# A decoder block on one core: weight buffers shared by both halves of the program, x loaded behind w_out, three down products accumulated in another's PSUM banks, a shorter row-norm chain

## The chip, the cores and the metric

The kernel runs on one core of one Trainium2 chip. The metric is the device time of one execution in microseconds (us); the time before is the median of three runs. A profile is one more execution, recorded by the hardware profiler. Its times are counted from the start of its span.

## The reference

One layer of a hybrid decoder on 512 tokens of width 1024, all in float32:

```python
h = rmsnorm(x, norm_attn_g)
q, k, v, u_pool, u_gate = split(h @ w_in)
a = diff_attention(q, k, v)          # 8 heads, rope, two softmaxes, w = p0 - lam * p1, rmsnorm per head
p = multiscale_pool(u_pool)          # causal means over 2, 4, 8, 16 tokens, then w_pool per group
merged = sigmoid(g_A) * a + sigmoid(g_P) * p
x = x + merged @ w_out
h2 = rmsnorm(x, norm_mlp_g)
x = x + square(relu(h2 @ w_up)) @ w_down        # 1024 -> 4096 -> 1024
return rmsnorm(x, final_norm_g)
```

## The kernel before

Every large product is made of three fp32r matmuls: each float32 operand is split into a rounded part (hi) and a rest (lo), and hi x hi, hi x lo and lo x hi are summed in PSUM. The weights come in tiles of 128 x 1024 float32 (512 KB, raw, `wr`), one DMA each on SP's queue (`get_w`, `load_w`). ScalarE casts a raw tile to its hi part `wh` (L109), then VectorE or GpSimd subtracts to get the lo part `wl` (L110). In the program's names a number behind a tile's name tells which one it is: `o0_2` is the third tile of the first half of w_out, `up0_3` the fourth w_up tile of quarter 0.

The order in which each engine takes its instructions is fixed when the program is built. A scheduler (`schedule_with_timeline_sim=True`) picks it from the dependences; tile pools decide which tiles share memory, and a tile that reuses memory waits for the last reader of the one before. Each engine, and SP's queue of DMA issues, works strictly in its order.

The stages, in order:
- The v projection, then attention: eight heads (`attn`), whose softmax chain runs over ScalarE and VectorE, with the gate projections (`ga`, `gp`) and the pooling as filler for TensorE. After each group of two heads `merge` applies the gates; its last step writes the merged tile as hi and lo part into `vh` and `vl` (L456, L457), which hold what w_out multiplies. The last group (heads 6 and 7) needs the last gate tile `gp7`, head 7's output `o7`, its norm (`ss`, L396, L397) and the pooled product `pp` (L451 to L453), whose weights `wpr` are loaded and split late; L454 takes pp out of PSUM.
- w_out, in two halves of 512 columns (n = 0 and 1, `po0` and `po1`), each of 8 x 3 matmuls for each of four token tiles t. Four weight tiles kk = 0 to 3 make up a half; tile kk covers heads 2 kk and 2 kk + 1. `x1_add` adds the result to x (L532) and squares it with a row sum (L514). After the second half come the row norm of h2 (L519, `rsqrt` L186 to L192, L553) and its transposes (L558), one token tile at a time.
- The MLP in four quarters q. `up(q)` has 8 weight tiles, each 24 matmuls; `down(q)` has 7 products of 24 matmuls in the order m1, m7, m6, m5, m2, m3, m4 (a Winograd-like scheme, whose weight operands `t1` to `t4` are sums of the loaded tiles, L629, and whose sums of results are made on VectorE in `accu` and in `x1`: U, V7 and V5 hold m1 + m6, m7 and m5 over the quarters).
- The final row norm, `finish` (L706), row by row in the last quarter, with output tiles `yo` from a pool tag `hy` of two buffers that squares and h2 use too.

Buffers for weights come from two pools. During attention `wp` has 3 raw tiles and 4 of hi and lo. `ctx1.close()` (L493) gives this memory and that of the attention tiles back, and a new pool `bk` takes it over, with 6 raw tiles and 4 of hi and lo (L495); its tiles wait for the old tiles in their place. The loads of x for the residual (L536) stand ahead of those of w_out.

Of the kernel before, what the change touches and what calls it, by code (L numbers as in the profile page):

```python
# [52 lines left out]
def block_kernel(ctx, tc, xT, x_tok, gains, pos, consts, w_in, w_v, w_pool, w_out, w_up, w_dn, out):  # L53
# [42 lines left out]
    def load_w(src, name, nsplit=1, parts=None):  # L96
        raw = wp.tile([P, 1024], F32, tag="wr", name=f"wr_{name}", bufs=wbufs[0])
        if nsplit == 1:
            nc.sync.dma_start(out=raw, in_=src)
# [409 lines left out]
    def hy(name):  # L509
        return bk.tile([P, D], F32, tag="hy", name=name, bufs=2)  # L510

    def square(t, n):

        A.activation(out=hy(f"sqj{t}_{n}")[:, :512], in_=x1[:, t, n * 512 : n * 512 + 512], func=AF.Square,  # L514
                     accum_out=st[:, t, n : n + 1])

    def row_scale(t):

        V.tensor_tensor(out=st[:, t, 2:3], in0=st[:, t, 0:1], in1=st[:, t, 1:2], op=ALU.add)  # L519
        rsqrt(st[:, t, 3:4], st[:, t, 2:3], st[:, t, 4:5], D)  # L520
        return st[:, t, 3:4]
# [25 lines left out]
    for t in range(NT):
# [5 lines left out]
        V.scalar_tensor_tensor(out=h2, in0=x1[:, t, :], scalar=row_scale(t), in1=g2b, op0=ALU.mult, op1=ALU.mult)  # L553
        for b in range(2):
            pt = acc(f"h2T{t}_{b}")
            for j in range(4):
                k = 4 * b + j
                T.transpose(out=pt[:, j * P : j * P + P], in_=h2[:, k * P : k * P + P], identity=ident)  # L558
# [50 lines left out]
    def down(q):  # L609
        def raw(b, name):  # L610
            out_ = []
            for c in range(2):
# [18 lines left out]
        def product(form, w, name, inner=True):
            pa = [acc(f"{name}{q}_{a}") for a in range(2)]
            order = [(p, a) for p in range(4) for a in range(2)] if inner else [(p, a) for a in range(2) for p in range(4)]
            for p, a in order:
# [3 lines left out]
                T.matmul(pa[a], lhsT=zh, rhs=hi[:, sl], start=p == 0, stop=False)  # L638
                T.matmul(pa[a], lhsT=zh, rhs=lo[:, sl], start=False, stop=False)  # L639
                T.matmul(pa[a], lhsT=zl, rhs=hi[:, sl], start=False, stop=p == 3)  # L640
            return pa

        def to_x1(pa, r, n, op=ALU.add):
            for a in range(2):
# [1 line left out]
                V.tensor_tensor(out=xs, in0=xs, in1=pa[a], op=op)  # L646

        def to_acc(pa, dst):
            for a in range(2):
                if q == 0:  # L650
                    A.copy(out=dst[:, a], in_=pa[a])
                else:
                    V.tensor_tensor(out=dst[:, a], in0=pa[a], in1=dst[:, a], op=ALU.add)
# [12 lines left out]
        for a in range(2):
            V.tensor_tensor(out=U[:, a], in0=m6[a], in1=U[:, a], op=ALU.add)
        comb(b12, b11, ALU.subtract)
        if last:
            for a in range(2):  # L670
                V.tensor_tensor(out=V7[:, a], in0=V7[:, a], in1=U[:, a], op=ALU.add)
            to_x1([V7[:, 0], V7[:, 1]], 1, 0)
        to_acc(product(S1, parts(b12, "t1", V), "m5"), V5)
        if last:
            for a in range(2):
                V.tensor_tensor(out=U[:, a], in0=U[:, a], in1=V5[:, a], op=ALU.add)
            to_x1([U[:, 0], U[:, 1]], 0, 1)
            for a in range(2):
                V.tensor_tensor(out=V7[:, a], in0=V7[:, a], in1=V5[:, a], op=ALU.add)
            to_x1([V7[:, 0], V7[:, 1]], 1, 1)  # L680
# [88 lines left out]
```

## Time and profile before

| | |
|---|---|
| median of three runs | 724.18 us (723.78 to 724.74) |
| profiled execution | 725.91 us, its span 724.1 us |
| mean granted TensorE clock | 0.981 |
| TensorE busy | 686.7 us (95%) in 3146 matmuls |
| VectorE, ScalarE, GpSimd busy | 516.8, 401.4, 276.0 us |
| HBM read | 70.94 MB, 101 GB/s over the span |

How to read what follows. A window's row gives its bounds and length, then the busy time and number of instructions of TensorE, its weight loads, VectorE, ScalarE and GpSimd, then the granted clock (1.00 is full), the share of the DMA engines, and GB/s. A timeline row gives the start, the duration, the engine, the line, the operation, the tiles out<-in, and in brackets how long the engine had idled and what ended that. PE is TensorE, PEld its weight loads, DVE VectorE, ACT ScalarE, POOL GpSimd, SPq SyncE's DMA queue; a line of groups has busy time and the mean ns of one behind the bar. In the waits, the total, the number and the longest stand behind the colon. Lines are those of the kernel before. Stages by time: v projection to 53 us, attention to 316, w_out with the row norm to 387, the MLP to 674 and on to its last matmul at 711.8, the final norm to 724.1.

### The profile page before, as it was taken

How to read it: one execution, taken by the hardware profiler on the slowest of the kernel's cores; microseconds unless marked ns; L12 is line 12 of the kernel's file. 1: busy time of each engine (PE TensorE's matmuls, PEld its weight loads, DVE VectorE, ACT ScalarE, POOL GpSimd, SP SyncE). 2: the span in 40 equal slices, each digit the busy share in tenths (PEclk: the TensorE clock that was granted, in tenths of full speed). 3: DMA queues.
4: the chain of work that ended last, by engine and by line, in shares of the span. 5: the costliest groups of instructions: out<-in, count | busy, mean ns of one | idle time of the engine just before them, and what ended most of it. 6: DMA issues, size and time to landing. Idle time of an engine off the chain costs nothing.

```text
span 724.1 us, 8745 instructions
## 1 busy us (share of the span) xinstructions
PE 686.7 (95%) x3146; PEld 567.1 (78%) x3146; DVE 516.8 (71%) x826; ACT 401.4 (55%) x661; POOL 276.0 (38%) x158
## 2 busy tenths in 40 slices
PE   8999999999999999967999999999999999999983
PEld 7888887787787877755888888888888888888872
DVE  6854998889899987945265886259833777259896
ACT  7553467874875768553355565356434564355424
POOL 6102623355335444404104314850465224850450
PEclk9999999999999999977999999999999999999997
DMA  8421322112311220056304314520264214520203
GB/s 269 161 103 58 117 84 82 48 61 81 100 59 58 79 75 0 2 215 233 110 31 123 110 58 155 194 88 30 88 209 151 76 59 149 197 90 29 88 30 117
DMA packets 22652, 73.61 MB, mean 102 GB/s; under 512 B 2768, under 2 KB 3408, under 8 KB 22608
## 3 DMA queue, kind: packets, MB, share of 16 engines
q1 hardware_dynamic: 22608, 73.05, 30.4%
q8 instruction: 25, 0.41, 0.2%
q14 instruction: 19, 0.16, 0.1%
HBM read 70.94 MB, written 2.10 MB: 101 GB/s over the span
## 4 chain that ended last, share of the span: by engine, by line
PE 57%; DVE 25%; ACT 10%; issue 4%; DMA 2%; POOL 2%; SPq 0%; DVEq 0%; ACTq 0%; POOLq 0%
PE pu L122 8%; PE pu L123 8%; PE pu L126 8%; PE m L639 6%; PE m L638 6%; PE m L640 6%; ACT p L367 2%; DVE p L372 2%; PE v L212 2%; PE v L213 2%; PE v L214 2%; PE po L527 2%; PE po L528 2%; DVE p L363 2%; PE po L526 2%
## 5 line engine op out<-in xcount | busy, mean ns | idle before, releaser
L110 POOL TENSOR_TENSOR wl_up<-wr_up,wh_up 128x1024 fp32r<-128x1024 f32 x30 | 74.3, 2481 | 75.6 <-ACT wh_up L109 60.1
L122 PE MATMUL pu<-x1gh,wh_up 128*128 128x512 f32 (+1 forms) x272 | 101.0, 377 | 0.2 <-ACT x1gh L561 0.2
L123 PE MATMUL pu<-x1gl,wh_up 128*128 128x512 f32 (+1 forms) x272 | 101.2, 377 | 0.0
L110 POOL TENSOR_TENSOR wl_t<-wr_b,wh_t 128x1024 fp32r<-128x1024 f32 x16 | 43.5, 2723 | 114.4 <-DVE zr L590 69.5
L126 PE MATMUL pu<-x1gh,wl_up 128*128 128x512 f32 (+1 forms) x272 | 63.8, 377 | 0.0
L122 PEld LDWEIGHTS pu<-x1gh,wh_up 128*128 128x128 f32 x272 | 51.0, 188 | 9.8 <-ACT x1gh L561 0.5
L123 PEld LDWEIGHTS pu<-x1gl,wh_up 128*128 128x128 f32 x272 | 51.1, 188 | 9.6 <-DVE x1gl L562 0.2
L367 ACT ACTIVATE p<-p,st 128x128 f32<-128x128 f32 (+3 forms) x64 | 35.7, 558 | 38.5 <-DVE st L363 38.2
L126 PEld LDWEIGHTS pu<-x1gh,wl_up 128*128 128x128 f32 x272 | 49.2, 188 | 9.3
L592 ACT CAST zfh<-zr 128x512 fp32r<-128x512 f32 (+1 forms) x32 | 30.3, 946 | 45.2 <-DVE zr L590 24.8
L629 DVE TENSOR_TENSOR wr_b<-wr_b,wr_b 128x1024 f32<-128x1024 f32 x32 | 48.0, 1507 | 5.7 <-DMA wr_b<-w_dn 5.5
L593 DVE TENSOR_TENSOR zfl<-zr,zfh 128x512 fp32r<-128x512 f32 (+1 forms) x32 | 38.5, 1203 | 18.0 <-ACT zfh L592 18.0
L109 ACT CAST wh_t<-wr_b 128x1024 fp32r<-128x1024 f32 x32 | 33.7, 1054 | 31.6 <-PE m L640 30.0
L109 ACT CAST wh_up<-wr_up 128x1024 fp32r<-128x1024 f32 x32 | 33.6, 1049 | 31.0 <-PE m L640 15.0
L639 PE MATMUL m<-wl_t,zfh 128*128 128x512 f32 x128 | 49.8, 389 | 0.0
L640 PE MATMUL m<-wh_t,zfl 128*128 128x512 f32 x128 | 49.8, 389 | 0.0
L638 PE MATMUL m<-wh_t,zfh 128*128 128x512 f32 x128 | 48.8, 389 | 0.0
L646 DVE TENSOR_TENSOR x<-x,m 128x512 f32<-128x512 f32 x30 | 20.2, 684 | 31.3 <-PE m L640 31.3
L639 PE MATMUL m<-wl_b,zfh 128*128 128x512 f32 x96 | 37.5, 390 | 2.4 <-DVE wl_b L110 2.4
L640 PE MATMUL m<-wh_b,zfl 128*128 128x512 f32 x96 | 37.4, 389 | 0.0
L638 PE MATMUL m<-wh_b,zfh 128*128 128x512 f32 x96 | 37.2, 389 | 0.0
L584 DVE TENSOR_TENSOR zr<-zr 128x256 f32<-128x256 f32 x16 | 15.6, 974 | 26.3 <-ACT zr L583 26.3
(257 smaller groups left out, 1874.0 us busy)
## 6 DMA issues: line engine op xcount, KB each, us to landing
wr_up<-w_up SPq DMA_DIRECT2D x32, 512.0 KB, 3.4
wr_b<-w_dn SPq DMA_DIRECT2D x32, 512.0 KB, 3.3
wr_q<-w_in SPq DMA_DIRECT2D x8, 512.0 KB, 3.3
wr_k<-w_in SPq DMA_DIRECT2D x8, 512.0 KB, 3.3
wr_ga<-w_in SPq DMA_DIRECT2D x8, 512.0 KB, 3.3
wr_gp<-w_in SPq DMA_DIRECT2D x8, 512.0 KB, 3.4
wr_o<-w_out SPq DMA_DIRECT2D x8, 512.0 KB, 6.5
wr_b22b<-w_dn SPq DMA_DIRECT2D x8, 512.0 KB, 3.3
```

The lines of the kernel that those rows point to most:

```text
L109: ins = A.copy(out=hi[:, sl], in_=raw[:, sl])
L110: (eng or G).tensor_tensor(out=lo[:, sl], in0=raw[:, sl], in1=f(hi)[:, sl], op=ALU.subtract)
L122: T.matmul(acc, lhsT=hi[:, c], rhs=rh[:, k, :], start=k == 0, stop=False)
L123: T.matmul(acc, lhsT=hi[:, c], rhs=rl[:, k, :], start=False, stop=False)
L126: T.matmul(acc, lhsT=lo[:, c], rhs=rh[:, k, :], start=False, stop=k == NK - 1)
L367: A.activation(out=pr[:, c, :N], in_=pr[:, c, :N], func=AF.Exp, scale=-1.0, bias=st[:, c : c + 1], accum_out=st[:, 2 + c : 3 + c])
L592: A.copy(out=zfh[:, sl, p, :], in_=F[:, sl])
L593: V.tensor_tensor(out=zfl[:, sl, p, :], in0=F[:, sl], in1=f(zfh)[:, sl, p, :], op=ALU.subtract)
L629: V.tensor_tensor(out=r1[c], in0=r1[c], in1=r2[c], op=op)
L638: T.matmul(pa[a], lhsT=zh, rhs=hi[:, sl], start=p == 0, stop=False)
L639: T.matmul(pa[a], lhsT=zh, rhs=lo[:, sl], start=False, stop=False)
L640: T.matmul(pa[a], lhsT=zl, rhs=hi[:, sl], start=False, stop=p == 3)
```

## The change

- The pool `wp` now lives to the end and serves both halves of the program, with 3 raw tiles and 4 of hi and lo. The w_down tiles `b12` and `b22`, which are combined in place, have four raw buffers of their own (`wr2`) in `bk`.
- The loads of x stand behind those of w_out's first half in the code.
- Three down products go on in the PSUM banks of another: m6 in m1's, m3 in m5's, m4 in m7's. So V7 and V5 are not needed: m1, m7 and m5 are added to x directly, the sum goes on in PSUM, and m4's sign is turned in its weights (`flip`). In the last quarter the splits of `b21` and `t4` are on VectorE.
- The row norm: for one half of the row the sum of squares is known early, and `row_early` makes of it a bias (two 128x1 operations); `row_scale` lets the logarithm take it, and the add of L519 goes. The squares' unused output goes into tiles that are there already; `hy` and `yo` go, `finish` works in place in x1, and of rows 2 and 3 the second half is multiplied by the gain ahead of time (VectorE) and scaled on ScalarE.

TensorE's order, at the end of attention. Before: the end of o7 (head 7's output), the sums of squares ss7 of its norm, the pooled products pp6 and pp7, then w_out's first half (`po0_0` is token tile 0):

```order
L384 MATMUL o7_2729<-wt_532,vh_107 128x128
L396 MATMUL ss7_2750<-sqh7_2744,onesr_88 128x512 [waits PE_49,Activation_49]
L397 MATMUL ss7_2750<-sql7_2746,onesr_88 128x512 [waits DVE_49]
L451 MATMUL pp6_2944<-dh3_2805,wt_532 128x512 [waits Activation_49]
L452 MATMUL pp6_2944<-dl3_2806,wt_532 128x512
L451 MATMUL pp7_2954<-dh3_2805,wt_532 128x512
L452 MATMUL pp7_2954<-dl3_2806,wt_532 128x512
L453 MATMUL pp6_2944<-dh3_2805,wt_532 128x512 [waits DVE_49]
L453 MATMUL pp7_2954<-dh3_2805,wt_532 128x512
L526 MATMUL po0_0_2976<-wh_o0_0_2982,vh_107 128x512 [waits DVE_49,Activation_49]
```

No matmul of w_out stood ahead of pp. Now, the same place (the lines are those of the changed kernel: L531 to L533 make po, L395 and L396 ss, L450 to L452 pp):

```order
L531 MATMUL po0_3_2975<-wh_o0_2_3038,vh_107 128x512
L395 MATMUL ss7_2750<-sqh7_2744,onesr_88 128x512 [waits PE_49,Activation_49]
L532 MATMUL po0_3_2975<-wl_o0_2_3039,vh_107 128x512
L533 MATMUL po0_3_2975<-wh_o0_2_3038,vl_108 128x512
L396 MATMUL ss7_2750<-sql7_2746,onesr_88 128x512 [waits DVE_49]
L450 MATMUL pp6_2944<-dh3_2805,wt_532 128x512 [waits Activation_49]
L451 MATMUL pp6_2944<-dl3_2806,wt_532 128x512
L450 MATMUL pp7_2954<-dh3_2805,wt_532 128x512
L451 MATMUL pp7_2954<-dl3_2806,wt_532 128x512
L452 MATMUL pp6_2944<-dh3_2805,wt_532 128x512 [waits DVE_49]
L452 MATMUL pp7_2954<-dh3_2805,wt_532 128x512
L531 MATMUL po0_0_2972<-wh_o0_0_2978,vh_107 128x512 [waits DVE_49]
```

All 36 matmuls of `po0_2` and `po0_3` with the tiles kk = 0 to 2 now stand ahead of pp, seven of them between gp7 and o7; behind pp come 36 of `po0_0` and `po0_1`, then the 24 with kk = 3.

SP's queue around the loads of x. Before: x, wpr (the last pooling weights), w_out's eight tiles with the gain between, then w_up:

```order
L536 DMA x1_2968<-x_tok 128x1024 [waits DMAHW1_49]
L431 DMA wpr3_2809<-w_pool 128x256 [waits DVE_49]
L99 DMA wr_o0_0_2980<-w_out 128x1024 [waits DMAHW4_49,DMAHW3_49,Activation_49]
L99 DMA wr_o0_1_3010<-w_out 128x1024
L99 DMA wr_o0_2_3040<-w_out 128x1024 [waits DMAHW5_49,Activation_49]
L99 DMA wr_o0_3_3070<-w_out 128x1024 [waits DMAHW6_49]
L505 DMA gain0_3112<-gains 128x1024 [waits DMAHW7_49,DVE_49,Pool_49]
L99 DMA wr_o1_0_3115<-w_out 128x1024 [waits DMAHW0_49]
L99 DMA wr_o1_1_3121<-w_out 128x1024 [waits DMAHW1_49]
L99 DMA wr_o1_2_3127<-w_out 128x1024 [waits DMAHW3_49,DMAHW2_49,Pool_49]
L99 DMA wr_o1_3_3133<-w_out 128x1024 [waits DMAHW4_49,DVE_49]
L99 DMA wr_up0_0_3343<-w_up 128x1024 [waits DMAHW5_49,Pool_49]
```

Now, from the sixth tile of w_out on; `wr_o0_0` to `wr_o1_0` stand ahead, behind the last load of attention:

```order
L98 DMA wr_o1_1_3125<-w_out 128x1024 [waits DMAHW0_49,Pool_49]
L547 DMA x1_2967<-x_tok 128x1024 [waits PE_49]
L547 DMA x1_2967<-x_tok 128x1024 x3
L98 DMA wr_o1_2_3131<-w_out 128x1024 [waits DMAHW1_49,DVE_49]
L430 DMA wpr3_2809<-w_pool 128x256
L503 DMA gain0_3116<-gains 128x1024 [waits DMAHW2_49,DVE_49]
L619 DMA wr_b120_0_3691<-w_dn 128x1024 [waits DMAHW3_49]
L619 DMA wr_b120_1_3693<-w_dn 128x1024 [waits DMAHW4_49,PE_49]
L619 DMA wr_b220_0_3695<-w_dn 128x1024 [waits DMAHW5_49,DVE_49]
L619 DMA wr_b220_1_3697<-w_dn 128x1024 [waits DMAHW6_49]
L98 DMA wr_o1_3_3137<-w_out 128x1024 [waits DMAHW7_49,Pool_49]
L98 DMA wr_up0_0_3335<-w_up 128x1024 [waits DMAHW0_49,DVE_49]
```

Six tiles of w_out moved ahead of x, one ahead of wpr, and the last, `wr_o1_3`, stands behind the gain and four w_down tiles, of which `wr_b220_0` waits for the write of the last `vl`.

VectorE in the last quarter, around the splits `wl_b22b` that m3 waits for. Before:

```order
L667 TENSOR_TENSOR accu_3342<-m63_1_5555,accu_3342 128x512 [waits DVE_49,PE_49]
L671 TENSOR_TENSOR accu_3342<-accu_3342 128x512 [waits DVE_49] x2
L646 TENSOR_TENSOR x1_2968<-x1_2968,accu_3342 128x512 [waits DVE_49] x2
L110 TENSOR_TENSOR wl_b223_0_5687<-wr_b22b3_0_5682,wh_b223_0_5686 128x1024 [waits DMAHW3_49,Activation_49]
L653 TENSOR_TENSOR accu_3342<-m53_0_5596,accu_3342 128x512 [waits PE_49]
L653 TENSOR_TENSOR accu_3342<-m53_1_5597,accu_3342 128x512 [waits PE_49]
L676 TENSOR_TENSOR accu_3342<-accu_3342 128x512 [waits DVE_49]
L679 TENSOR_TENSOR accu_3342<-accu_3342 128x512
L676 TENSOR_TENSOR accu_3342<-accu_3342 128x512 [waits DVE_49]
L679 TENSOR_TENSOR accu_3342<-accu_3342 128x512
L110 TENSOR_TENSOR wl_b223_1_5691<-wr_b22b3_1_5684,wh_b223_1_5690 128x1024 [waits DMAHW4_49,Activation_49]
```

Now:

```order
L670 TENSOR_TENSOR accu_3334<-m13_1_5413,accu_3334 128x512 [waits PE_49]
L652 TENSOR_TENSOR x1_2967<-accu_3334,x1_2967 128x512 [waits DVE_49]
L652 TENSOR_TENSOR x1_2967<-accu_3334,x1_2967 128x512
L652 TENSOR_TENSOR x1_2967<-accu_3334,x1_2967 128x512 [waits DVE_49]
L652 TENSOR_TENSOR x1_2967<-accu_3334,x1_2967 128x512
L109 TENSOR_TENSOR wl_b213_1_5573<-wr_b213_1_5566,wh_b213_1_5572 128x1024 [waits Activation_49]
L109 TENSOR_TENSOR wl_b223_0_5617<-wr_b22b3_0_5612,wh_b223_0_5616 128x1024 [waits DMAHW3_49,Activation_49]
L652 TENSOR_TENSOR x1_2967<-m53_0_5524,x1_2967 128x512 [waits PE_49]
L652 TENSOR_TENSOR x1_2967<-m53_1_5525,x1_2967 128x512 [waits PE_49]
L109 TENSOR_TENSOR wl_b223_1_5621<-wr_b22b3_1_5614,wh_b223_1_5620 128x1024 [waits DMAHW4_49,Activation_49]
```

The operations from `accu` to `accu` (L671, L676, L679) are gone, adds from `accu` into x1 stand in their place, and `wl_b213_1` came in: the splits of `b21` and `t4` in this quarter were GpSimd's and are VectorE's now.

The diff, cut to its core:

```diff
-    wp = ctx1.enter_context(tc.tile_pool(name="wp", bufs=1))
+    wp = ctx.enter_context(tc.tile_pool(name="wp", bufs=1))
...
-        raw = wp.tile([P, 1024], F32, tag="wr", name=f"wr_{name}", bufs=wbufs[0])
+        raw = wp.tile([P, 1024], F32, tag="wr", name=f"wr_{name}", bufs=3)
...
-    wp, wbufs = bk, (6, 4)
...
+    def square(t, n, junk):
+
+        A.activation(out=junk, in_=x1[:, t, n * 512 : n * 512 + 512], func=AF.Square, accum_out=st[:, t, n : n + 1])
+
+    def row_early(t, n):
+
+        V.tensor_scalar(out=st[:, t, 2:3], in0=st[:, t, n : n + 1], scalar1=1.0 / D, scalar2=EPS, op0=ALU.mult, op1=ALU.add)
+        V.tensor_scalar(out=st[:, t, 3:4], in0=st[:, t, n : n + 1], scalar1=D * EPS, scalar2=None, op0=ALU.add)
+
+    def row_scale(t, n):
+
+        src, r, u = (st[:, t, i : i + 1] for i in (n, 4, 5))
+        A.activation(out=r, in_=src, func=AF.Ln, scale=1.0 / D, bias=st[:, t, 2:3])
+        A.activation(out=r, in_=r, func=AF.Exp, scale=-0.5)
+        A.activation(out=u, in_=r, func=AF.Square, scale=1.0 / math.sqrt(D))
+        V.scalar_tensor_tensor(out=u, in0=src, scalar=st[:, t, 3:4], in1=u, op0=ALU.add, op1=ALU.mult)
+        V.scalar_tensor_tensor(out=r, in0=u, scalar=-3.0, in1=r, op0=ALU.add, op1=ALU.mult)
+        return r
...
-    for t in range(NT):
-        nc.sync.dma_start(out=x1[:, t, :], in_=x_tok[t])
     po = [acc(f"po0_{t}") for t in range(NT)]
...
     for t in range(NT):
+        nc.sync.dma_start(out=x1[:, t, :], in_=x_tok[t])
+    for t in range(NT):
         x1_add(t, 0, po[t])
+        row_early(t, 0)
...
-        def product(form, w, name, inner=True):
-            pa = [acc(f"{name}{q}_{a}") for a in range(2)]
+        def product(form, w, name, onto=None, inner=True, stop=True):
+
+            pa = onto or [acc(f"{name}{q}_{a}") for a in range(2)]
...
+        Us = [U[:, a] for a in range(2)]
+        b11 = raw(0, "b11", "wr", wp)
...
+        b12, x_ = raw(1, "b12", "wr2", bk), raw(3, "b22", "wr2", bk)
+        m1 = product(A11, w1, "m1", stop=False)
         to_x1(m1, 0, 0)
         comb(x_, b12, ALU.subtract)
+        m7 = product(S3, parts(x_, "t3", V), "m7", stop=False)
+        to_x1(m7, 1, 1)
         comb(x_, b11, ALU.add)
+        m6 = product(S2, parts(x_, "t2", G), "m6", onto=m1)
         for a in range(2):
+            if q == 0:
+                A.copy(out=Us[a], in_=m6[a])
+            else:
+                V.tensor_tensor(out=Us[a], in0=m6[a], in1=Us[a], op=ALU.add)
         comb(b12, b11, ALU.subtract)
+        m5 = product(S1, parts(b12, "t1", V), "m5", stop=False)
+        to_x1(m5, 1, 1)
         if last:
+            for r, n in ((1, 1), (0, 1), (1, 0)):
+                to_x1(Us, r, n)
             for t in (2, 3):
+                square(t, 1, yr[:, 0])
+                row_early(t, 1)
+        b21 = raw(2, "b21", "wr", wp)
+        to_x1(product(A12, parts(b21, "b21", V if last else G), "m2"), 0, 0)
...
+        comb(x_, b21, ALU.subtract, flip=True)
+        m3 = product(S4, parts(raw(3, "b22b", "wr", wp), "b22", V), "m3", onto=m5)
         to_x1(m3, 0, 1)
         if last:
+            for t in (2, 3):
+                V.tensor_tensor(out=x1[:, t, 512:], in0=x1[:, t, 512:], in1=gfb[:, 512:], op=ALU.mult)
             for t in (0, 1):
+                square(t, 1, yr[:, 1])
+                finish(t, 1)
+        m4 = product(A22, parts(x_, "t4", V if last else G), "m4", onto=m7, inner=not last)
...
+            V.tensor_tensor(out=xs, in0=m4[a], in1=xs, op=ALU.add)
+            square(2 + a, 0, yr[:, 0])
+            finish(2 + a, 0)
+
+    def finish(t, n):
+
+        r = row_scale(t, n)
+        for i in (0, 1):
+            xs, gs = x1[:, t, i * 512 : i * 512 + 512], gfb[:, i * 512 : i * 512 + 512]
+            if n == 0 and i == 1:
+                A.activation(out=xs, in_=xs, func=AF.Copy, scale=r)
+            else:
+                V.scalar_tensor_tensor(out=xs, in0=xs, scalar=r, in1=gs, op0=ALU.mult, op1=ALU.mult)
+            nc.sync.dma_start(out=out[t, :, i * 512 : i * 512 + 512], in_=xs)
```

More of the change, by code (lines that the diff above doesn't have):

```diff
@@ L507, in gain @@
         return g
[L509 to L521, printed above, removed]
+    h2 = bk.tile([P, NT, D], F32, tag="zfl", name="h2", bufs=1)
+    def square(t, n, junk):
[11 more added lines that the diff above has]
+        return r
     def mm_rows(a_, t, k, w, start, stop):
@@ L532, in x1_add @@
         V.tensor_tensor(out=xs, in0=a_, in1=xs, op=ALU.add)
-        square(t, n)
-    for t in range(NT):
-        nc.sync.dma_start(out=x1[:, t, :], in_=x_tok[t])
+        square(t, n, h2[:, t, :512])
     po = [acc(f"po0_{t}") for t in range(NT)]
@@ L557, in block_kernel @@
                 k = 4 * b + j
-                T.transpose(out=pt[:, j * P : j * P + P], in_=h2[:, k * P : k * P + P], identity=ident)
+                T.transpose(out=pt[:, j * P : j * P + P], in_=h2[:, t, k * P : k * P + P], identity=ident)
             pv = pt.rearrange("p (j q) -> p j q", q=P)
@@ L568, in block_kernel @@
     zfh = bk.tile([P, 7, 4, HS], F32R, name="zfh")
-    zfl = bk.tile([P, 7, 4, HS], F32R, name="zfl")
+    zfl = bk.tile([P, 7, 4, HS], F32R, tag="zfl", name="zfl", bufs=1)
     zr = big.tile([P, 2, 8, HS], F32, tag="s3", name="zr")
     accu = big.tile([P, 4, 2, 512], F32, tag="s2", name="accu")
-    U, V7, V5 = (accu[:, i] for i in range(3))
+    U, yr = accu[:, 0], accu[:, 1]
     def up_mm(a_, w, t0, t1):
@@ L641, in product, with to_x1 @@
+                T.matmul(pa[a], lhsT=zl, rhs=hi[:, sl], start=False, stop=p == 3 and stop, skip_group_check=True)
             return pa
-        def to_x1(pa, r, n, op=ALU.add):
+        def to_x1(pa, r, n):
             for a in range(2):
                 xs = x1[:, 2 * r + a, n * 512 : n * 512 + 512]
[L646 to L653, printed above, removed]
+                V.tensor_tensor(out=xs, in0=pa[a], in1=xs, op=ALU.add)
@@ L669, in down @@
+        to_x1(m5, 1, 1)
         if last:
[L670 to L680, printed above, removed]
+            for r, n in ((1, 1), (0, 1), (1, 0)):
+                to_x1(Us, r, n)
@@ L691, in down @@
+        comb(x_, b21, ALU.subtract, flip=True)
+        m3 = product(S4, parts(raw(3, "b22b", "wr", wp), "b22", V), "m3", onto=m5)
         to_x1(m3, 0, 1)
         if last:
+            for t in (2, 3):
+                V.tensor_tensor(out=x1[:, t, 512:], in0=x1[:, t, 512:], in1=gfb[:, 512:], op=ALU.mult)
             for t in (0, 1):
-                square(t, 1)
-                finish(t)
-        m4 = product(A22, parts(x_, "t4", G), "m4", inner=not last)
+                square(t, 1, yr[:, 1])
+                finish(t, 1)
```

55 lines of the change are left out of this document (15 added, 40 removed).

## The prediction

> **What bounds the kernel now.** I read the busy time by stage, then the waits of TensorE.
>
> ```profile
> 53.00:316.00 263.00, 254.35 (x1213) 209.90 (x1211) 222.46 (x449) 171.51 (x335) 108.60 (x74) 1.00 0.20 64
> 316.00:387.00 71.00, 59.81 (x279) 48.71 (x280) 36.57 (x49) 30.74 (x58) 17.55 (x7) 0.88 0.48 166
> 387.00:671.00 284.00, 283.76 (x1276) 235.65 (x1275) 176.43 (x193) 146.38 (x176) 117.04 (x46) 1.00 0.34 111
> 671.00:724.10 53.10, 38.47 (x169) 31.21 (x167) 45.36 (x60) 21.25 (x41) 18.15 (x6) 0.90 0.21 77
> ```
>
> ```profile
> PE po L526 <- ACT wh_o L109: 4.5, 1, 4.5
> PE ss L396 <- ACT sqh L390: 3.3, 1, 3.3
> PE m L639 <- DVE wl_b L110: 2.4, 1, 2.4
> ```
>
> TensorE (the first busy column) is the bound. From 387 to 671 it idles 0.24 us, so nothing is to be won there: the change keeps every matmul. Idle time lies in 316 to 387 (11.2 us, with the granted clock, third column from the right, at 0.88) and after 671 (14.6 us). The waits put names to it: the first two lie where attention ends and w_out begins, the third in the last quarter. The first place, in windows of 2 us and in the timeline:
>
> ```profile
> 316.00:318.00 2.00, 0.00 (x0) 0.00 (x0) 0.00 (x0) 1.97 (x3) 1.26 (x1) 0.98 1.00 397
> 328.00:330.00 2.00, 0.00 (x0) 0.00 (x0) 1.92 (x4) 1.61 (x3) 0.00 (x0) 0.50 0.07 6
> 334.00:336.00 2.00, 2.00 (x8) 1.56 (x7) 2.00 (x2) 0.35 (x1) 2.00 (x1) 0.75 1.08 293
> ```
>
> ```profile
> 314.96 0.81 PE L384 MATMUL o<-wt,vh 128*128 128x512 f32 x4
> 315.73 0.44 SPq L431 DMA_DIRECT2D wpr<-w_pool  x1
> 316.28 2.33 SPq L99 DMA_DIRECT2D wr_o<-w_out  x4
> ...
> 322.70 0.40 ACT L434 CAST wt<-wpr 128x256 fp32r<-128x256 f32 x1 [1.13 <-DMA wpr<-w_pool]
> 323.16 0.80 PE L451 MATMUL pp<-dh,wt 128*128 128x512 f32 x1 [2.32 <-ACT wt L434]
> ...
> 327.01 0.75 DVE L454 SCALAR_TENSOR_TENSOR g<-pp,con,g 128x512 f32<-128x512 f32 x1
> 329.04 1.29 DVE L457 TENSOR_TENSOR vl<-o,vh 128x512 fp32r<-128x512 f32 x2
> 330.60 2.08 PE L526 MATMUL po<-wh_o,vh 128*128 128x512 f32 x4 [4.51 <-ACT wh_o L109]
> 330.63 5.71 POOL L110 TENSOR_TENSOR wl_o<-wr_o,wh_o 128x1024 fp32r<-128x1024 f32 x2 [12.71 <-ACT wh_o L109]
> ...
> 335.20 0.40 PE L528 MATMUL po<-wh_o,vl 128*128 128x512 f32 x1
> ...
> 353.11 0.39 PE L527 MATMUL po<-wl_o,vh 128*128 128x512 f32 x1
> ```
>
> o7's last matmul ends at 315.8; from there to 335.2 TensorE does 8 matmuls of the merge and 9 of w_out, at half clock in the middle window and at 0.75 in the last. Warm, matmuls follow one another by 0.2267 us: from 335.20 to 353.11 there are 79 of them without a gap. The w_out loads go out only at 316.28, behind x and wpr, and their casts stand on ScalarE behind the merge.
>
> **The first hole.** Shared buffers let w_out load during attention, and the scheduler puts 36 matmuls of po_2 and po_3 around o7, ahead of pp (w_out's rows of heads 0 to 5 need no late merge). From 315.8: 36 x 0.2267 = 8.2 gives 324.0; two ss, 0.5, give 324.5. pp waits for wpr, which now has wr_o1_2's 512 KB ahead: at the 397 GB/s of 316 to 318 that is 1.3 us, so its cast starts near 324.0 instead of 322.70 and pp, 0.46 later as before, at 324.5: just in time. Six pp take 1.4 (325.9). po_0 takes pp6's bank, so it waits for L454 (0.75) and starts near 326.9, 1 us idle. The 60 matmuls left of n = 0 take 13.6: 340.5. Before, 87 are left at 335.20: 354.9. That is 14.4 won. The clock should stay: 53 to 316 holds 8.7 us of idle in short pieces at 1.00. The merge's last step, vl, ended at 330.3; with po_0's and po_1's 36 matmuls of kk 0 to 2 ahead, it is asked for at 335.1, so a merge 2 us later is hidden, and past 4.8 it would cost.
>
> Against it stand the casts and splits moved into attention:
>
> ```profile
> 292.64 1.62 POOL L419 TENSOR_TENSOR pb<-pa 128x512 f32<-128x512 f32 x1
> 293.38 0.90 DVE L370 TENSOR_TENSOR st<-st,lvec 128x2 f32<-128x2 f32 x1
> ...
> 296.38 0.15 DVE L370 TENSOR_TENSOR st<-st,lvec 128x2 f32<-128x2 f32 x1
> ```
>
> ```profile
> 296.00:300.00 4.00, 3.42 (x17) 2.74 (x18) 3.95 (x13) 2.17 (x6) 0.31 (x1) 1.00 0.02 4
> ```
>
> VectorE is full there, with the softmax of h = 7 on which TensorE's in-order queue waits. Two splits of w_out come on VectorE, two on GpSimd (2.86 each, by the 5.71 for two). The 128x2 step of the softmax chain shows what GpSimd does to it: 0.90 where a GpSimd row runs beside it, 0.15 where none does. Bounds: nothing, if all falls into gaps and GpSimd's empty time (0.31 busy of 4); 5.7, if both GpSimd splits hold the chain up whole. I take 1.5: a block of 0.75, as in that row, for each of the two. **Term: 14.4 - 1.5 = 12.9.**
>
> Weighed against a rule: the Trainium skill, SBUF — State Buffer, section Who interferes with whom, says that a VectorE instruction with two SBUF inputs and a GpSimd one that reads SBUF share a read port as an exclusive lock, and whoever comes second blocks for the whole of the other. The 0.90 agrees in kind, not in full length. By the rule at its worst the term would be 14.4 - 5.7 = 8.7.
>
> **The tail.**
>
> ```profile
> 670.94 0.39 PE L638 MATMUL m<-wh_b,zfh 128*128 128x512 f32 x1
> 696.81 5.74 POOL L110 TENSOR_TENSOR wl_t<-wr_b,wh_t 128x1024 fp32r<-128x1024 f32 x2 [4.59 <-ACT wh_t L109]
> 696.82 0.68 DVE L679 TENSOR_TENSOR accu<-accu 128x512 f32<-128x512 f32 x1
> 700.24 2.87 DVE L679 TENSOR_TENSOR accu<-accu 128x512 f32<-128x512 f32 x1
> 703.02 1.21 DVE L110 TENSOR_TENSOR wl_b<-wr_b22b,wh_b 128x1024 fp32r<-128x1024 f32 x1
> 711.45 0.39 PE L640 MATMUL m<-wh_t,zfl 128*128 128x512 f32 x1
> 712.70 0.68 DVE L702 TENSOR_TENSOR x<-x,m 128x512 f32<-128x512 f32 x1
> 717.50 0.63 ACT L514 ACTIVATE sqj<-x 128x512 f32<-128x512 f32 x1 [1.21 <-DMA out<-yo]
> 719.63 1.41 DVE L711 SCALAR_TENSOR_TENSOR yo<-x,st,gain 128x512 f32<-128x512 f32 x2
> ```
>
> 167 spacings of 0.2267 from 670.94 give 708.8 for the last matmul; it starts at 711.45, and the wait of 2.4 for wl_b is most of that. wl_b stood behind an add of 2.9 (L679), which takes 0.68 where it gets in ahead of GpSimd's split. Adds and GpSimd splits go (the splits to VectorE, 1.2 each), so TensorE should not wait. VectorE then has x<-m3, rows 0 and 1 and four output halves to do after m3's end (703.7): my walk along its queue, 0.68 an add and 1.2 a split, ends x<-m4 of the last row at 712.0, where the row at 712.70 ended at 713.4. From there to the end of the last output write were 719.63 + 1.41 - 713.4 = 7.6 us, with waits for yo buffers (1.21 in one). Now nothing waits for yo: square and its read 0.8, row 2's scaling on ScalarE 0.6 ahead of Ln, three 128x1 steps 0.8, two more on VectorE 0.4, the two halves side by side 0.7: 3.3, so 715.3, and the store and end as now (724.1 - 721.0 = 3.1): 718.4. **Term: 5.7**, between 4 (VectorE 1.7 later) and 6.5 (row 2 not in the way).
>
> **What could come late elsewhere.**
>
> ```profile
> wr_up<-w_up SPq DMA_DIRECT2D x32, 512.0 KB, 3.4
> wr_o<-w_out SPq DMA_DIRECT2D x8, 512.0 KB, 6.5
> ```
>
> ```profile
> L109 ACT CAST wh_up<-wr_up 128x1024 fp32r<-128x1024 f32 x32 | 33.6, 1049 | 31.0 <-PE m L640 15.0
> L110 POOL TENSOR_TENSOR wl_up<-wr_up,wh_up 128x1024 fp32r<-128x1024 f32 x30 | 74.3, 2481 | 75.6 <-ACT wh_up L109 60.1
> ```
>
> Second half of w_out: before, its weights kept ahead (the only waits of po L526 are the 4.5 above). Now wr_o1_3 stands on SP's queue behind the gain and four w_dn loads, one of which waits for the last vl, by now near 332; at the 6.5 of crowded w_out loads it lands at 338.5. po_0 ends at 340.5, two adds and a square (2.0) go ahead on ScalarE, cast 1.05, split 1.2 to 2.9: 344.8 to 346.5. It is needed 37 matmuls (8.4) after 340.5, at 348.9. Slack 2.4: cost 0, up to 5 for the range.
>
> Row chain ahead of the first up phase:
>
> ```profile
> 381.42 0.90 DVE L519 TENSOR_TENSOR st<-st 128x1 f32<-128x1 f32 x1 [0.79 <-ACT sqj L514]
> 386.24 1.09 PE L558 MATMUL h2T<-ident,h 128*128 128x128 f32 x8 [0.62 <-DVE h L553]
> ```
>
> L519 goes from the last row's chain, 0.9, but only TensorE's wait of 0.62 can be won, and the chain's other 128x1 steps may still be held by GpSimd's splits. Bounds 0 and 0.62: **0.2**.
>
> The three products that go on in others' banks wait for VectorE's add into x1 instead of an own bank; one product (5.44) at least lies between, two adds of 0.68 fit: 0. The adds that go there were hidden.
>
> **Sum.** 12.9 + 0.2 + 5.7 = 18.8. The profiled execution took 725.91, 1.8 more than its span of 724.1; the median of the runs is 724.18. I take the difference from the median: **705.4**.
>
> **Rivals.** (1) *GpSimd blocks the softmax:* 5.7 in place of 1.5, 709.6. For: VectorE full, the add of 2.9 in the tail; against: 0.75 in attention's own row. It is the page's rule at full price (the Trainium skill, as above). 0.13. (2) *w_out's second half starves:* if wr_o1_3 lands after about 341, the wait for wh_o1_3 takes the place of the one removed: 2 to 5 us, 707.4 to 710.4. For: an in-order queue with a late wait ahead; against: 2.4 of slack. 0.15. (3) *The hole stays* (the change doesn't do what it does on paper): if po_3's weights are late, the early matmuls only push o7 back, or the clock falls anyway, row chain and tail alone count: 718.3. 0.12. (4) *Slower:* three raw buffers starve the up phases. A buffer's turn is 3.4 + 1.05 + 2.5 = 6.9; TensorE asks for a tile each 24 x 0.2267 = 5.44, for the same buffer each 16.3. It decides only above that; to lose 18.8 over 29 tiles each must come 0.65 late, a turn of 18.3; at 18.7, 29 x 0.8 = 23 are lost: 728. 0.04.
>
> **Numbers.** Forecast 0.56: 702.5 to 707.5 (hole 11 to 14.4, tail 4 to 6.5, row chain to 0.62). Rivals 1 and 2 lie within 712 with the tail's low end; 702 to 712 leaves out rivals 3 and 4 and 0.04 of the rest. 0.2%, 1.45 us, is about what a measurement of this kernel can tell from no change (the runs lie 723.78 to 724.74). Faster 0.95, same 0.01, slower 0.04.
>
> **What would show it.** Right: po matmuls around o7 and no window of clock 0.50 from 314 to 340; pp6's L454 the last wait there; the stage of 387 to 671, shifted, as full; no wait on wl_b in the last quarter; squares of the last rows without a DMA ahead; 3 to 3.5 us from the last x<-m4 to the last output row. Wrong: po waiting on wh_o1_3 (rival 2), longer VectorE rows and TensorE waits on p near 296 to 312 (rival 1), clock 0.50 after o7 (rival 3), pu waiting on wh_up (rival 4).

## The result and the profile after

The changed kernel takes 708.52 us (median of four runs, 707.67 to 708.90) where the kernel before, run again beside it, takes 724.46 (four runs, 723.78 to 725.16): a ratio of 0.978, 95% interval 0.976 to 0.980. It is 15.9 us faster; 705.4 was forecast, 3.1 less. 708.52 lies in the whole range given, 702 to 712, but above the 702.5 to 707.5 of the forecast itself, near rival 1's 709.6 and inside rival 2's 707.4 to 710.4. Its profiled execution took 708.77 us with a span of 706.8.

The time by stage, of the changed kernel (windows, columns as before; w_out now runs from about 317 to 374, the last quarter's down products start at 660):

```profile
53.00:300.00 247.00, 236.32 (x1124) 195.32 (x1123) 212.14 (x424) 160.22 (x315) 108.67 (x73) 1.00 0.22 75
300.00:316.00 16.00, 16.00 (x66) 12.93 (x65) 12.70 (x24) 10.26 (x21) 4.72 (x3) 0.85 0.16 49
316.00:345.00 29.00, 28.39 (x128) 23.13 (x127) 15.23 (x23) 16.11 (x22) 6.66 (x3) 1.00 0.67 238
374.00:656.00 282.00, 281.05 (x1270) 233.66 (x1269) 190.87 (x189) 141.20 (x170) 121.61 (x46) 1.00 0.34 113
656.00:706.80 50.80, 42.47 (x188) 34.85 (x186) 41.28 (x64) 24.52 (x46) 5.72 (x2) 0.94 0.21 73
```

The hole behind o7 is closed: TensorE idles 0.6 us in the 29 from 316 to 345, at full clock. But the 16 us ahead of it, where it is busy throughout, ran at a mean clock of 0.85; that loss was not there before. The waits of TensorE say where it comes from. The long waits for wh_o, sqh, wt and wl_b are gone, and the longest single one is new:

```profile
PE t L375 <- DVE pa L423: 2.9, 1, 2.9
PE h2T L563 <- DVE h L558: 0.7, 1, 0.7
PE po L531 <- DVE g L453: 0.6, 1, 0.6
```

The timeline of the changed kernel at that wait and behind o7:

```profile
294.87 2.41 POOL L109 TENSOR_TENSOR wl_o<-wr_o,wh_o 128x1024 fp32r<-128x1024 f32 x1
294.99 2.31 DVE L369 TENSOR_TENSOR st<-st,lvec 128x2 f32<-128x2 f32 x1
295.38 0.29 PE L375 MATMUL t<-ident,p 128*128 128x128 f32 x1
298.57 0.66 PE L375 MATMUL t<-ident,p 128*128 128x128 f32 x2 [2.90 <-DVE pa L423]
300.30 0.63 PE L121 MATMUL gp<-xh,wh_gp 128*128 128x512 f32 x1
...
317.31 0.39 PE L531 MATMUL po<-wh_o,vh 128*128 128x512 f32 x1
...
327.95 0.51 PE L450 MATMUL pp<-dh,wt 128*128 128x512 f32 x1
330.23 0.50 PE L531 MATMUL po<-wh_o,vh 128*128 128x512 f32 x1 [0.61 <-DVE g L453]
```

GpSimd's split of w_out's first tile, moved in here, and VectorE's 128x2 step of head 7's softmax end together, at 297.3: the step, 0.15 us at this place before, took 2.31. (The wait is put down to L423, the row that VectorE finished last.) The clock rows behind the wait, of the changed kernel:

```profile
296.00:298.00 2.00, 0.00 (x0) 0.00 (x0) 1.97 (x3) 0.51 (x1) 1.28 (x1) 0.95 0.00 0
298.00:300.00 2.00, 1.43 (x5) 1.27 (x6) 1.98 (x6) 0.86 (x2) 0.00 (x0) 0.50 0.70 258
300.00:302.00 2.00, 2.00 (x6) 1.53 (x5) 1.97 (x6) 1.87 (x6) 0.33 (x1) 0.50 0.05 12
304.00:306.00 2.00, 2.00 (x9) 1.57 (x9) 1.82 (x5) 1.90 (x5) 0.07 (x1) 0.84 0.00 0
```

Half clock until about 305: six matmuls in two microseconds where ten stand from 306 to 308. In the profile this stretch is 4.95 us longer than before, measured from the first matmul of gate tile ga6 to the first behind gp7 (34.17, from 283.14 to 317.31; before 29.21, from 284.53 to 313.74). This execution is one of the dearer ones: of the four runs, the two with a mean granted clock of 0.991, this one among them, took 708.77 and 708.90, the two with 0.995 took 708.27 and 707.67. Three kernels below have the same order of matmuls in this stretch (the last quarter's splits back on GpSimd, the row chain of before, both output halves on VectorE); in their profiles it took 32.94, 32.73 and 32.89, so 3.5 to 3.7 more than before.

The row chain ahead of the first up phase, changed kernel. A cast of a w_up tile now stands ahead of the last row's square:

```profile
369.17 0.69 DVE L537 TENSOR_TENSOR x<-po,x 128x512 f32<-128x512 f32 x1
369.93 1.05 ACT L108 CAST wh_up<-wr_up 128x1024 fp32r<-128x1024 f32 x1 [1.92 <-DMA wr_up<-w_up]
370.88 0.62 ACT L511 ACTIVATE h<-x 128x512 f32<-128x512 f32 x1
...
372.43 1.46 DVE L524 SCALAR_TENSOR_TENSOR st<-st 128x1 f32<-128x1 f32 x1 [2.57 <-ACT st L523]
```

And its end; the last matmul, the last row's result, its square without a DMA ahead, and the two halves of the row side by side:

```profile
698.08 0.39 PE L646 MATMUL m<-wh_t,zfl 128*128 128x512 f32 x1
699.07 0.68 DVE L702 TENSOR_TENSOR x<-m,x 128x512 f32<-128x512 f32 x1
699.79 0.63 ACT L511 ACTIVATE accu<-x 128x512 f32<-128x512 f32 x1 [0.40 <-DVE x L702]
702.26 0.72 ACT L712 ACTIVATE x<-x,st 128x512 f32<-128x512 f32 x1 [0.48 <-DVE st L525]
702.26 0.75 DVE L714 SCALAR_TENSOR_TENSOR x<-x,st,gain 128x512 f32<-128x512 f32 x1
```

The sum by the two profiles, each term the difference of two distances between the same instructions: 1.4 before ga6 and so ahead of what changed (the two executions are 1.4 apart by 27 us already, in the v projection; 725.91 was 1.5 over the median), -4.95 in attention, +14.5 from gp7 to the end of w_out's first half (41.2 to 26.6), -0.25 in the second half and the row chain, 0 in the four quarters up to the last down phase, +2.65 there (no wait for wl_b), +3.9 behind the last matmul (12.65 to 8.72): 17.3, the difference of the spans. Without the first it is 15.9, the difference of the medians.

### The profile page after: what moved, and what is told of

Same layout as the page of the kernel before. It is cut to its first block, busy times and chain, and to the rows that moved or that the text cites. A ratio compares the mean times of both kernels' runs of the same rounds, so it can differ in the third digit from the quotient of the medians.

```text
span 706.8 us, 8712 instructions
## 1 busy us (share of the span) xinstructions
PE 683.5 (97%) x3146; PEld 565.7 (80%) x3146; DVE 527.2 (75%) x828; ACT 399.5 (57%) x659; POOL 267.9 (38%) x154
## 4 chain that ended last, share of the span: by engine, by line
PE 61%; DVE 23%; ACT 10%; issue 4%; POOL 1%; DMA 1%; SPq 0%; ACTq 0%; DVEq 0%
PE pu L121 8%; PE pu L122 8%; PE pu L125 8%; PE m L644 7%; PE m L646 7%; PE m L645 7%; ACT p L366 2%; DVE p L371 2%; PE po L531 2%; DVE p L362 2%; PE po L533 2%; PE po L532 2%; DVE qs L342 2%; DVE st L369 2%; PE v L213 1%
## 5 line engine op out<-in xcount | busy, mean ns | idle before, releaser
L109 POOL TENSOR_TENSOR wl_up<-wr_up,wh_up 128x1024 fp32r<-128x1024 f32 x30 | 80.1, 2679 | 73.5 <-ACT wh_up L108 60.6
L634 DVE TENSOR_TENSOR wr_b<-wr_b,wr_b 128x1024 f32<-128x1024 f32 x32 | 68.7, 2155 | 12.5 <-DMA wr_b<-w_dn 12.4
L109 POOL TENSOR_TENSOR wl_t<-wr_b,wh_t 128x1024 fp32r<-128x1024 f32 x14 | 36.7, 2621 | 107.7 <-DVE zr L595 65.6
L598 DVE TENSOR_TENSOR zfl<-zr,zfh 128x512 fp32r<-128x512 f32 (+1 forms) x32 | 36.8, 1149 | 24.4 <-ACT zfh L597 24.4
L652 DVE TENSOR_TENSOR x<-m,x 128x512 f32<-128x512 f32 x46 | 30.1, 681 | 9.3 <-PE m L646 9.3
L348 POOL TENSOR_TENSOR ks<-q1k,kz 64x512 fp32r<-64x512 f32 x16 | 24.8, 1550 | 21.9 <-ACT kz L345 21.3
```

What stands on the lines that cost most here:

```text
L109: (eng or G).tensor_tensor(out=lo[:, sl], in0=raw[:, sl], in1=f(hi)[:, sl], op=ALU.subtract)
L598: V.tensor_tensor(out=zfl[:, sl, p, :], in0=F[:, sl], in1=f(zfh)[:, sl, p, :], op=ALU.subtract)
L634: V.tensor_tensor(out=r1[c], in0=(r2 if flip else r1)[c], in1=(r1 if flip else r2)[c], op=op)
```

## The experiments

Theory A: GpSimd's split wl_o0_0 holds VectorE's 128x2 step, TensorE waits, and the clock falls behind the wait. Theory B, its rival: the casts and VectorE's splits that were moved into attention cost it, or its order does. All times below are medians beside the kernel before of the same chip (724.67 to 725.59 in the three sets). The changed kernel was not run again in these sets, so a difference to its 708.52 of about 1 us or less is read from traces, not from the times.

**The split two places later on GpSimd.**

```diff
+        raw_, *w = load_w(w_out[0, kk], f"o0_{kk}")
+        A.copy(out=w[0], in_=raw_)
+        sp_ = (V if kk % 2 else G).tensor_tensor(out=w[1], in0=raw_, in1=f(w[0]), op=ALU.subtract)
+        if kk == 0:
+            after(sp_, sqls[6])
```

> The changed kernel, with one GpSimd instruction two places later: the split wl_o0_0 stands behind the two operations on head 6's squares instead of ahead of them; every other engine's order is as it was. Theory A (the split holds VectorE's 128x2 step L369 for 2.3 us, TensorE waits 2.9 us for head 7's second transpose and falls to half clock until 305): the wait falls to about 0.5, no window of 0.50 from 294 to 312, and of the 4.9 us lost there 4.5 to 5 come back: 703.5 to 704.3. Theory B (what was moved into attention on ScalarE and VectorE, casts and splits, costs the 4.9): the casts stay where they were, the wait stays near 2.9: 708.5. If the split now holds up a later VectorE step in the same way: 706 to 708.

704.12 (703.52 to 704.68); ratio to before 0.971 (0.969 to 0.973). One instruction two places later on one engine gives 4.4 us back. Its timeline and its wait:

```profile
294.59 0.15 DVE L370 TENSOR_TENSOR st<-st,lvec 128x2 f32<-128x2 f32 x1
301.48 2.73 POOL L545 TENSOR_TENSOR wl_o<-wr_o,wh_o 128x1024 fp32r<-128x1024 f32 x1
```

```profile
PE t L376 <- DVE pa L424: 0.8, 1, 0.8
```

The step takes 0.15 again, the wait is 0.8 (0.5 was expected), the clock rows from 294 to 306 are 1.00, and from ga6's first matmul to the first behind gp7 it is 29.2 us, as before the change. Theory A holds; the casts, in the same places, cost nothing that shows.

**The same split alone, in the kernel before.** A subtraction of two 128x1024 operands into a dead tile, on GpSimd at that place.

```diff
-            G.tensor_tensor(out=a, in0=a, in1=sa, op=ALU.mult)
+            g_ = G.tensor_tensor(out=a, in0=a, in1=sa, op=ALU.mult)
+            if h == 5:
+                after(G.tensor_tensor(out=kzs[0], in0=f(xl)[:, 0:2, :], in1=f(xl)[:, 2:4, :], op=ALU.subtract), g_)
```

> The kernel before, with one GpSimd subtraction more, of two 128x1024 SBUF operands, into a dead tile, behind head 5's gate product; nothing else moves on any engine. Theory A: it costs by itself what the change lost there, a wait of 2 to 3 us on head 7's second transpose and a stretch at half clock: 724.4 + 4.9 = 729.3 (at least 727 if only the wait comes). Theory B: GpSimd has room there, nothing happens: 724.4.

728.97 (727.33 to 729.83), ratio 1.005 (1.004 to 1.007): 4.1 more than the 724.88 beside it. The subtraction and the step held by it, the wait and the clock of this run:

```profile
295.31 2.41 POOL L450 TENSOR_TENSOR kz<-xl 128x1024 fp32r<-128x1024 f32 x1
295.43 2.31 DVE L370 TENSOR_TENSOR st<-st,lvec 128x2 f32<-128x2 f32 x1
```

```profile
PE t L376 <- DVE pa L424: 2.7, 1, 2.7
```

```profile
300.00:302.00 2.00, 2.00 (x6) 1.56 (x5) 2.00 (x6) 1.87 (x6) 0.00 (x0) 0.50 0.05 12
```

So the GpSimd instruction needs nothing else of the change to cost its price.

**The split on VectorE.**

```diff
-        w = get_w(w_out[0, kk], f"o0_{kk}", V if kk % 2 else None)
+        w = get_w(w_out[0, kk], f"o0_{kk}", None if kk == 2 else V)
```

> The changed kernel with the split wl_o0_0 on VectorE in place of GpSimd. Theory A (the block by GpSimd was the loss): the wait of 2.9 and the half clock go, and VectorE, full there, gets 1.2 us of work: between 703.6 (hidden) and 705 (1.2 to 1.4 late). Rival (any split in this stretch makes TensorE wait over 2 us and lose its clock): 707.5 to 708.5.

703.85 (703.24 to 704.59), ratio 0.971 (0.969 to 0.973). VectorE, full there by its busy time, took 1.2 us of work more without TensorE waiting for it: its wait at that place is 0.5.

**How much of it is the clock.** Ten extra matmuls in the wait, whose results are overwritten.

```diff
             t_ = tbk(f"t{h}_{i}")
+            if h == 7 and i == 1:
+                for _ in range(10):
+                    after(T.matmul(t_, lhsT=xh[:, 0, 0:P], rhs=xh[:, 0, :], start=True, stop=True), tr_)
```

> The changed kernel, with ten extra warm matmuls (2.3 us) into head 7's transpose bank between its first and second transpose, where TensorE waits 2.9 us; their results are overwritten. GpSimd's split stays. Theory A with two parts (2.2 us of wait, 2.75 us of half clock behind it): the wait stays, the clock stays at 1.00, 2.75 come back: 705.8. Rival (behind the wait VectorE's softmax steps set the pace, not TensorE's clock): no gain, 708 to 708.5, or slower if the matmuls hold the queue.

708.01 (706.92 to 708.87), ratio 0.977: its median is not told from the changed kernel's. The scheduler had moved two matmuls of head 7's scores up, and in the profiled run (708.87) the clock fell all the same, later, as two of its rows show (a wait of 0.56 and one of 1.05 lay 2 us apart ahead of it):

```profile
298.00:300.00 2.00, 0.91 (x4) 0.47 (x4) 1.98 (x6) 0.80 (x2) 0.00 (x0) 1.00 0.69 260
302.00:304.00 2.00, 2.00 (x6) 1.52 (x6) 1.46 (x3) 1.43 (x5) 1.92 (x2) 0.50 0.00 0
```

Its four runs differ: the two with a mean granted clock of 0.997, that of the kernel with the later split (0.996 to 0.998), took 706.92 and 707.23, the two with 0.993 and 0.995 took 708.87 and 708.78. So the two with the higher clock were 1.5 to 2 us faster. To part the clock from the moved order, it was done again with the order on TensorE held by dependences (the scores behind gp6's third product with the low part, head 6's sum and head 7's third transpose in their places of before in gate 7's products). Head 6's second sum and head 7's last transposes still stand nine and three matmuls off their old places.

> As the kernel with the ten extra matmuls, with TensorE's order around head 7's scores, transposes and head 6's sums held as it was in the changed kernel (in the first try the scores moved ahead and TensorE waited 1.05 us for them later, with the clock at 0.50 in 302 to 304 again). Theory A in two parts: clock at 1.00 all through, 2.75 back, 705.8. Rival (VectorE's softmax steps set the pace behind the wait, so the half clock is hidden under them): 707.5 to 708.5.

707.95 (706.51 to 708.21), ratio 0.976: the time alone doesn't decide. In its profile (706.51) the clock is 1.00 throughout, and from ga6's first matmul to the first behind gp7 it is 31.33 us, from 282.46 to 313.79, where the changed kernel's profile has 34.17 and the kernel with the later split 29.22. So 2.84 of the 4.95 were the clock, 2.1 the wait, close to the 2.75 and 2.2 expected. Against the three profiles of 32.7 to 32.9 above the clock's part is 1.4 to 1.6; the wait's 2.1 stays. But the end of the stretch is not the end of its cost: 1.2 of it went to a wait for wpr's cast ahead of pp,

```profile
PE pp L464 <- ACT wt L442: 1.2, 1, 1.2
```

and of its five runs two lie at 706.5 to 706.6 and three at 708.0 to 708.2. The clock alone does not set them apart (0.997 in the first two, 0.998, 0.998 and 0.993 in the others); what does stays open.

**The last quarter's splits back on GpSimd.**

```diff
-        to_x1(product(A12, parts(b21, "b21", V if last else G), "m2"), 0, 0)
+        to_x1(product(A12, parts(b21, "b21", G), "m2"), 0, 0)
...
-        m4 = product(A22, parts(x_, "t4", V if last else G), "m4", onto=m7, inner=not last)
+        m4 = product(A22, parts(x_, "t4", G), "m4", onto=m7, inner=not last)
```

> The changed kernel with the last quarter's four splits (b21 and t4) back on GpSimd. If it was GpSimd's splits that held VectorE's adds and with them wl_b, TensorE waits 1 to 2.5 again and the adds into x take up to 2.9: 710 to 711.5. Rival (the adds that went, not the splits, freed VectorE): the time stays within 0.5: 708 to 709.

708.15 (707.64 to 708.47), ratio 0.977: no difference, the rival was right. The block is there, on four adds into x (first row, this kernel; second row, the changed one), and nobody waits for it:

```profile
677.00 5.54 DVE L652 TENSOR_TENSOR x<-accu,x 128x512 f32<-128x512 f32 x4
```

```profile
678.31 2.48 DVE L652 TENSOR_TENSOR x<-accu,x 128x512 f32<-128x512 f32 x4
```

TensorE has no wait for wl_b. So it was not the moved splits that took that wait away. That leaves the adds that went with the products accumulated in one bank; no run put these back.

**No sharing: the second half's buffers in the new pool, x ahead of w_out.**

```diff
-    wp = ctx.enter_context(tc.tile_pool(name="wp", bufs=1))
+    wp = ctx1.enter_context(tc.tile_pool(name="wp", bufs=1))
...
+    wp = bk
```

> The changed kernel with the weight buffers of the second half in the new pool again and x loaded ahead of w_out, as before; tail, row norm and accumulation stay changed. Theory A: the hole is as before, its 14.5 are gone and the 4.9 lost in attention come back: 708.5 + 9.6 = 718.1, with a wait of po for wh_o near 4.5, the clock at 0.50 behind o7, and no wait of 2.9 on head 7's transpose. Rival (the shared buffers cost later what they win, in the up phases): 712 to 715.

718.46 (717.86 to 718.95), ratio 0.991 (0.989 to 0.992). The hole is back with the wait of before, and the block in attention is gone (0.5 at head 7's transpose):

```profile
PE po L532 <- ACT wh_o L108: 4.5, 1, 4.5
PE t L375 <- DVE pa L423: 0.5, 1, 0.5
```

The sharing with its earlier loads is worth 9.9 net, the rest of the change 6.2 (724.67 to 718.46).

**The row chain of before in the changed kernel.**

```diff
+        V.tensor_tensor(out=st[:, t, 2:3], in0=st[:, t, 0:1], in1=st[:, t, 1:2], op=ALU.add)
+        r = st[:, t, 3:4]
+        rsqrt(r, st[:, t, 2:3], st[:, t, 4:5], D)
```

> The changed kernel with the row norm chain of before: the add of the two halves' sums, then the logarithm; without the two early 128x1 operations. If the shorter chain is worth its 0.16 and the handover of 0.2 in the last row, the time rises by 0.4: 708.9. Ahead of the first up phase the wait for h2's last transposes, 0.71 after and 0.62 before, should then be longer, up to 0.5 more: 709.4 in all. Rival: the chain is hidden by other steps on VectorE (the early operations cost as much as the add): 708.5.

710.87 (709.85 to 710.99), ratio 0.980 (0.978 to 0.982): 2.3 more than the changed kernel, over five times the 0.4. The two intervals of the ratio overlap a little, so the trace has to say where it lies. Ahead of the first up phase its add of two 128x1 operands ran into GpSimd's split of a w_up tile, and TensorE waited 1 us more:

```profile
370.94 2.16 DVE L519 TENSOR_TENSOR st<-st 128x1 f32<-128x1 f32 x1 [1.87 <-ACT h L511]
...
375.75 1.06 PE L559 MATMUL h2T<-ident,h 128*128 128x128 f32 x8 [1.70 <-DVE h L554]
```

Another 1.1 lies behind the last matmul (9.82 to the end of the span, 8.72 in the changed kernel). There GpSimd held nothing up: its last instruction had ended at 670.6, and the last row's add took 0.16:

```profile
667.26 3.31 POOL L109 TENSOR_TENSOR wl_t<-wr_b,wh_t 128x1024 fp32r<-128x1024 f32 x1 [0.29 <-POOL wl_t L109]
700.97 0.16 DVE L519 TENSOR_TENSOR st<-st 128x1 f32<-128x1 f32 x1 [0.59 <-ACT accu L511]
```

From the last row's result to its last output write it is 3.62, 0.36 more than in the changed kernel, as expected for the chain. Most of the rest lies behind that write (4.4 to the end of the span, against 3.7): here the steps of the last two rows stand side by side, and their four stores go out one behind the other from 702.97. That is another order, not a longer chain.

**Both output halves on VectorE.** In `finish` the branch for ScalarE and the two multiplications ahead of it are left out.

```diff
-            if n == 0 and i == 1:
-                A.activation(out=xs, in_=xs, func=AF.Copy, scale=r)
-            else:
-                V.scalar_tensor_tensor(out=xs, in0=xs, scalar=r, in1=gs, op0=ALU.mult, op1=ALU.mult)
+            V.scalar_tensor_tensor(out=xs, in0=xs, scalar=r, in1=gs, op0=ALU.mult, op1=ALU.mult)
```

> The changed kernel with both halves of every output row made on VectorE again (no multiplication by the gain ahead, no scaling on ScalarE), still in place. If the halves side by side are what shortened the end of the last row, it takes 0.7 longer: 709.2. If the gain after the last matmul (3.9) came from the output buffers that nobody waits for any more, the time stays: 708.5; VectorE has two multiplications less, and the last row could even come 0.3 sooner.

707.48 (706.91 to 707.80), ratio 0.975 (0.973 to 0.977), not told from the changed kernel; behind the last matmul its span goes on for 8.54, against 8.72. The halves side by side are not what shortened the end: from the last row's result to its last write they take 3.26 in the changed kernel and 3.45 here, but from there to the end of the span it is 3.7 there and 3.1 here, where the first half's store goes out before the second half is written.

**The cast of w_up's fourth tile behind the last row's steps, with the split on VectorE.**

```diff
+                raw, *wu[m] = load_w(w_up[q * 8 + m], f"up{q}_{m}")
+                cast = split_w(raw, *wu[m])
+                if (q, m) == (0, 3):
+                    after(cast, chain[3])
```

> The kernel with wl_o0_0 on VectorE (703.9), and ScalarE's cast of w_up's fourth tile moved behind the last row's square and logarithm steps, which it stood ahead of; nothing else moves but one DMA issue by a place. Theory: the cast (1.05), not the chain's own length, kept the row chain from gaining; the wait for h2's last transposes falls from 0.7 to near 0 and GpSimd's second split no longer holds the 128x1 step L524: 703.1 to 703.3. Rival: the transposes' wait is set by the third row's work on ScalarE and VectorE, no change: 703.9. The interval of the time is as wide as the difference, so the trace decides: L524 of the last row at 0.2 instead of 1.46, and the wait.

702.73 (702.33 to 703.15), ratio 0.969 (0.966 to 0.971), the lowest median of all; the interval overlaps that of the kernel with the split on VectorE, so the trace decides. The square follows the add at once, and the 128x1 step takes 0.22 instead of 1.46:

```profile
364.40 0.68 DVE L539 TENSOR_TENSOR x<-po,x 128x512 f32<-128x512 f32 x1
365.12 0.63 ACT L511 ACTIVATE h<-x 128x512 f32<-128x512 f32 x1 [1.88 <-DVE x L539]
...
366.68 0.22 DVE L526 SCALAR_TENSOR_TENSOR st<-st 128x1 f32<-128x1 f32 x1 [1.59 <-ACT st L525]
```

Its list of TensorE's waits has none for h2's transposes any more. From the last matmul of w_out's first half to the first of the first down phase it is 70.77, where the kernel with the split on VectorE has 71.74, the changed kernel 71.68 and the kernel before 71.44.

## Why the prediction was right, and where it was off

**The hole itself: right.** 14.4 was worked out for it, 14.5 came. TensorE did 36 matmuls of w_out around o7, pp's weights were there in time (no wait ahead of 327.95), the last wait was po_0's for L453 (0.61, 1 us was expected), and the clock stayed at 1.00.

**The step that failed: "Bounds: nothing ... 5.7 ... I take 1.5: a block of 0.75, as in that row, for each of the two."** The block came, at one of the two splits, and cost 4.4 by the times (4.95 in the profile): the 128x2 step started 0.12 us behind the split and was held for all of it, 2.31 and not 0.75. The row that the price was taken from, 0.90 beside a GpSimd row of 1.62, was a step that came in the middle of one. The second split, wl_o0_2, ran later (311.68) and TensorE did not wait. That was rival 1, put at 0.13; it got the place and the mechanism right, and its 709.6 is nearer to the 708.5 measured than the forecast. That the number came so near is partly luck: it took two blocks, each as long as a split; there was one block, and half clock made up for the other. "The clock should stay: 53 to 316 holds 8.7 us of idle in short pieces at 1.00" failed with it: those pieces were at most 1.4 us long, and 2.9 was enough to lose the clock. The Trainium skill's SBUF — State Buffer, Who interferes with whom, weighed there as the worst case, describes what was found: whoever comes second is blocked for the whole of the other. The kernel before with one GpSimd instruction more, and the split two places later, show that case from both sides.

**Row chain: 0.2 forecast, -0.25 measured.** The sign came from an instruction that the sum left out, the cast of w_up's fourth tile, which the new order put ahead of the last row's square. Removing the add was worth more than said, about 1 us here, because in the new timing that add would have met GpSimd's split (2.16 where it takes 0.16 alone); the cast and a block of L524 took it back. With the cast moved the wait is gone, as the last experiment shows, and from w_out's first half to the first down phase it is then 0.67 shorter than before, about the upper bound of 0.62 that was given.

**Second half of w_out: right.** wr_o1_3 was issued at 339.6, cast at 346.7 and split by 349.0; TensorE asked for it about 352 and did not wait. Rival 2 did not come. The hole did not stay (rival 3), and the four quarters took as long as before (rival 4: up to the last down phase, the distance between the starts of two down phases is 81.6 in both).

**Tail: 5.7 forecast, 6.6 measured, partly for another reason.** The wait for wl_b went as forecast (2.65), but the sentence that gave GpSimd's splits as its cause was half wrong: with the splits back on GpSimd the wait does not return. What is left as the cause is the adds that went, by exclusion. From the last row's add to its last output write it was 3.3, as worked out (7.7 before), and here the gain behind the last matmul lies; that add ended 1.7 us behind the start of the last matmul, not 3.2, since VectorE had been ahead; the store took 3.7 to the end of the span, not 3.1. These two misses go against each other, so that 6.6 lies near 5.7 is in part luck. Neither the splits nor ScalarE's half shortened the end, and the chain's add is worth 0.4 of it, by the kernel with the old chain. That the outputs in place, with no yo buffer to wait for, made the rest is argued from the two waits of before that are gone (0.68 and 1.21 ahead of squares); it was not tried alone.

The sum: 14.5 - 4.95 - 0.25 + 6.6 = 15.9, where 14.4 - 1.5 + 0.2 + 5.7 = 18.8 stood.

## What to carry to other kernels

What filling the hole would bring came out to 0.1 us; what went wrong is what the moved work does to the place that it now runs in. Before a GpSimd instruction is moved, look for VectorE steps with two SBUF operands next to it, however small, that others wait for: price them at the whole length of the GpSimd instruction, and the matmuls behind at half clock if TensorE then stands still for as long as the 2.7 to 2.9 us here. Where one queue place decides, move it by one or two places, or to the other engine, before anything else is changed: here that was worth 4.4 us more.
